# A hybrid HGRN2 / mLSTM block: where the sums and splits of the FFN operand stand, and where the HGRN stream pauses

## The chip, the cores and the metric

The kernel runs on one core of a Trainium2 chip. The core has four compute engines, each with a queue of its own that it works through in order: TensorE (PE, matrix products into PSUM banks), VectorE (DVE), ScalarE (ACT) and GpSimd (POOL). SyncE (SP) and ACT issue most DMAs. The engines wait for each other by semaphores. The metric is the time of one launch on the device in microseconds; less is better.

## The reference

One layer (DEPTH is 1) over 1024 tokens of width 1024, all in float32:

```
u = x @ w_in + b_in                       # columns split between two head groups
o_hg = rms(hgrn2(silu(hq), log_f, k, hv)) * silu(hgate)     # 4 heads, 128 x 128 state
o_ml = rms(mlstm(mq, mk, mv, ig, log_f))  * sigmoid(mo)     # 4 heads, qk 64, v 128
mix = concat(o_hg, o_ml) @ w_out
x = LN(alpha * x + mix)
ffn = (silu(x @ w_gate) * (x @ w_up)) @ w_down              # D_FF = 2816
x = LN(alpha * x + ffn)
x = x + sigmoid(x @ ple_gate + b) * (p @ ple_proj)
```

## The kernel before

**Three products for one.** A float32 product is made from two reduced halves. `split` (lines 82 to 84) rounds an operand to its high half on ACT (a cast) and takes the low half on DVE (operand minus high half). `mm3` (lines 86 to 90) then runs three matmuls, high x high (L88), high x low or low x high (L89, L90). Nearly all of PE's time lies in these three lines, and each operand costs one ACT cast and one DVE subtraction ahead of its first use.

**Stages.** `mixers` makes the projections tile by tile (`f_tile`, 2 x 24 matmuls of 512 columns into the `ft` banks) and runs the recurrences in between: generators, the "streams", hold the HGRN and the mLSTM work, and `pump` advances each stream to its next `yield` twice for every 24 matmuls. `out_proj` multiplies by w_out, normalises (`ln_rows`), transposes the result (`transposed`, PE transposes into `pt`, ACT writes `x1T`), and makes the small product p @ ple_proj (`ple_proj`: products `pp`, copied to `ppo`, sent to DRAM). `ffn_up` and `ffn_down` are the FFN.

**The HGRN stream.** `hgrn(h, b, ...)` handles head h and half b of the tokens. It makes q1 (line 527), the scores of neighbouring tokens (L533), then doubles the block length L from 2 to 64; at each length a `yield`, score products (L533 up to 16, L549 for 32 and 64), and then DVE scales q and k (L570, L571) by the decay of the block. After L = 64 come two `yield`s, the transposes of k (`pkt`, L579), the state products (`hst`, L585), the output (`po`, L599, L601), the normalisation (`rms`, which leaves `onh`), five `yield`s marked "tail", and the transposes of the output (L607). `together` runs both halves in step. `head(h)` calls `finish(head_streams[h - 1], 'tail')` after its two projections, which emits all that the former head has left up to the first "tail" at once. A head has 8 pumps between its start and that point. The score products and `po` share three PSUM banks ("hg").

**The FFN in seven products.** `ffn_up` forms the products of the 2 x 2 block matrix of x (a11, a12: the first 512 tokens, columns halves 0 and 1; a21, a22: the last 512 tokens) with sums of the weights, after Strassen and Winograd: z with A11 and A12, y with S3 and A22, x with S1 and S4, w with S2. S1 = a21 - a22, S2 = S1 - a11 (sign as in the code), S3 = a11 - a21, S4 = a12 + S2. `xs(name)` makes a sum and its split when it is first asked for; S3 is asked for ahead of the loop over the 22 weight tiles. The first four tiles' z products are made early in `out_proj` (`gate0`): z with A11, a copy to `p1` on ACT, then z goes on with A12 on the same bank, so its second half waits for that copy.

**What sets the order.** The program text is not the order of the queues: a scheduler of the tile framework places the instructions of each engine by their dependencies and by its own estimate of times. So a moved line moves its neighbours too, and the order of the built kernel is shown below where the prediction speaks of it.

Of the kernel before, what the change touches and what calls it, by code (L numbers as in the profile page):

```python
# [9 lines left out]
F32 = mybir.dt.float32  # L10
# [3 lines left out]
OP = mybir.AluOpType  # L14
# [4 lines left out]
P = 128  # L19
# [6 lines left out]
HB = 512  # L26
# [15 lines left out]
A11, A12, A22, S1, S2, S3, S4 = range(7)  # L42
# [7 lines left out]
def block_kernel(ctx, tc, a, out):  # L50
# [81 lines left out]
    with ff:  # L132
        with ExitStack() as es:
            ffn_up(g, es)
# [4 lines left out]
def mixers(g, es):  # L139
    a, act, dve, pool, pe, sp = g.a, g.act, g.dve, g.pool, g.pe, g.sp  # L140
# [30 lines left out]
    for k in range(KT):  # L171
# [7 lines left out]
        for b in range(2):  # L179
            raw = mtile("xraw")  # L180
            sp.dma_start(raw, a["xT"][:, k, b * HB:(b + 1) * HB])
            xraw.append(raw)
    for k in range(KT):
# [5 lines left out]
        for b in range(2):  # L189
            raw = xraw[2 * k + b]  # L190
# [196 lines left out]
    def rms(tag, views, scale_r):  # L387
        sq = mx.tile([P, 4, P], F32, name="sq", bufs=1)
        for sl, v in views:
            act.activation(sq[:, sl], v, AF.Square)  # L390
        ss = mx.tile([P, 4], F32, name="ss" + tag)
        dve.tensor_reduce(ss, sq, axis=AX.X, op=OP.add)
        if scale_r is not None:
            dve.tensor_mul(ss, ss, scale_r)
            dve.tensor_mul(ss, ss, scale_r)
        dve.tensor_scalar(ss, ss, 1.0 / P, RMS_EPS, op0=OP.mult, op1=OP.add)
        rs = mx.tile([P, 4], F32, name="rs" + tag)
        pool.tensor_tensor(rs, ss, g.m8[:, :4], op=OP.pow)
        if scale_r is not None:
            dve.tensor_mul(rs, rs, scale_r)  # L400
        on = mx.tile([P, 4, P], F32, name="on" + tag, bufs=1)
        for sl, v in views:
            n = len(range(4)[sl])
            dve.tensor_mul(on[:, sl], v, rs[:, sl][:, :, None].to_broadcast([P, n, P]))
        return on
# [106 lines left out]
    def hgrn(h, b, q, k, f):  # L512
        v = mx.tile([P, 4, P], F32, name="hv")
        sp.dma_start(v, g.hv_d[4 * b:4 * b + 4, :, h * P:(h + 1) * P].rearrange("c p d -> p c d"))
        k, f = (t.rearrange("p (c t) -> p c t", c=4) for t in (k, f))
# [6 lines left out]
        def odd(t):  # L522
            return t.rearrange("p c (b two) -> p c b two", two=2)[:, :, :, 1]

        A = Ab[b]
        D = mx.tile([P, 4, BK], F32, name="D")
        dve.tensor_mul(q1, odd(q), odd(f))

        def blocks(dst, rhs, n):
            for c in range(4):  # L530
                for j in range(NB):
                    s = slice(j * BK, (j + 1) * BK)
                    pe.matmul(dst[s, c], k[:, c, s], rhs[:, c, j * n:(j + 1) * n], start=True, stop=True)  # L533
# [66 lines left out]
            if prev is not None:  # L600
                pe.matmul(po[:, c], q[:, c], prev, start=False, stop=True)  # L601
        on = rms("h", [(slice(0, 4), po)], None)
        for _ in range(5):
            yield "tail"
        pt = bank("hg", [P, 4, P], "pt")
        for c in range(4):
# [33 lines left out]
def out_proj(g, es):  # L640
    a, act, dve, pool, pe, sp = g.a, g.act, g.dve, g.pool, g.pe, g.sp
    wtile, mm3, split = g.wtile, g.mm3, g.split
    lnp = es.enter_context(g.tc.tile_pool(reuse_waits="tile", name="lnp", bufs=2))
    ps = g.psC
    g.x1T = {}

    def acc_bank(name):
        return ps.tile([P, 512], F32, tag="q", bufs=8, name=name)

    mixhl = []  # L650
    for b in range(2):
        mixhl.append((g.big("mixh"), g.big("mixl")))
        for k in KORD:
            split(mixhl[b][0][:, k], mixhl[b][1][:, k], g.mix[k, b])

    g.ft = ffn_tools(g, acc_bank)
    g.early = {}

    def ple_proj(b, pw, pT):
        ph, pl = (t[:, :1024].rearrange("p (k t) -> p k t", k=2) for t in pT)  # L660
        for t in range(4):
            tt = slice(t * P, (t + 1) * P)
            for s in range(2):
                pp = acc_bank("pp")
                for k in range(2):
                    ks = slice(k * HB, (k + 1) * HB)
                    mm3(pp, (ph[:, k, tt], pl[:, k, tt]), tuple(w[:, ks] for w in pw[s]), k == 0, k == 1)
                r = g.wp.tile([P, HB], F32, name="ppo", bufs=2)
                act.copy(r, pp)
                act.dma_start(g.pp_d[4 * b + t, :, s * HB:(s + 1) * HB], r)  # L670

    def wo(b, s):
        mh, ml = mixhl[b]
        accs = [acc_bank(f"wo{t}") for t in range(4)]
        for i, k in enumerate(KORD):
            if i % 2 == 0:
                hi, lo = wtile(a["wo"][s, k // 2])
            ks = slice((k % 2) * HB, (k % 2 + 1) * HB)
            for t in range(4):
                tt = slice(t * P, (t + 1) * P)  # L680
                mm3(accs[t], (mh[:, k, tt], ml[:, k, tt]), (hi[:, ks], lo[:, ks]), i == 0, i == KT - 1)
        return accs

    def add_up(ys, s, accs):
        for t in range(4):
            hs = slice(s * HB, (s + 1) * HB)
            dve.scalar_tensor_tensor(ys[t][:, hs], ys[t][:, hs], ALPHA, accs[t], op0=OP.mult, op1=OP.add)

    def rows(b):
        ys = [lnp.tile([P, D], F32, name="y", bufs=4) for _ in range(4)]  # L690
        for t in range(4):
            act.dma_start(ys[t], a["x"][(4 * b + t) * P:(4 * b + t + 1) * P])
        return ys

    def transposed(b, ys):
        for k in range(KT):
            pt = ps.tile([P, 4, P], F32, tag="q", bufs=8, name="pt")
            for t in range(4):
                pe.transpose(pt[:, t], ys[t][:, k * P:(k + 1) * P], g.ident)
            g.x1T[k, b] = g.mtile(f"x1T{k}")  # L700
            act.activation(g.x1T[k, b], pt.rearrange("p c t -> p (c t)"), AF.Identity,
                           bias=g.ln1c[:, 1, k:k + 1], scale=g.ln1c[:, 0, k:k + 1])
        for t in range(4):
            act.dma_start(g.x1_d[4 * b + t], ys[t])

    y0 = rows(0)
    for s in range(2):
        add_up(y0, s, wo(0, s))
    for t in range(4):
        g.ln_rows(y0[t], lnp)  # L710
    accs = wo(1, 0)
    transposed(0, y0)
    y1 = rows(1)
    add_up(y1, 0, accs)
    g.X = {"A11": x_split(g, g.big("XA11"), 0, 0), "A12": x_split(g, g.big("XA12"), 4, 0)}
    accs = wo(1, 1)
    w0 = [g.ft.prep0(f) for f in range(2)]
    g.early[0] = g.ft.gate0(w0[0])
    pw = [wtile(a["wpp"][s]) for s in range(2)]
    ple_proj(0, pw, wtile(a["pT"][0]))  # L720
    w0.append(g.ft.prep0(2))
    add_up(y1, 1, accs)
    for t in range(4):
        g.ln_rows(y1[t], lnp)
    transposed(1, y1)
    pT = wtile(a["pT"][1])
    for f in range(1, 3):
        g.early[f] = g.ft.gate0(w0[f])
    ple_proj(1, pw, pT)
    g.early[3] = g.ft.gate0(g.ft.prep0(3))  # L730


def x_split(g, t, k0, b, raw=None):
    for k in range(4):
        g.split(t[:, k], t[:, 4 + k], raw[k] if raw else g.x1T[k0 + k, b])
    return t


# [45 lines left out]
def ffn_up(g, es):  # L784
    a, act, dve, sp = g.a, g.act, g.dve, g.sp
    cb = es.enter_context(g.tc.tile_pool(reuse_waits="tile", name="cb", bufs=3))
    tp = es.enter_context(g.tc.tile_pool(reuse_waits="tile", name="tp", bufs=1))
    bank = lambda name: g.psC.tile([P, HB], F32, tag="q", bufs=8, name=name)
    T, X, t = g.ft, g.X, g.x1T

    def cbt(name):
        return cb.tile([P, KT, HB], F32R, tag="cb", bufs=3, name=name)

    def row(k0, b):
        return [t[k0 + k, b] for k in range(4)]

    def comb(dst, x, y, op):
        for k in range(4):
            dve.tensor_tensor(dst[k], x[k], y[k], op=op)
        return dst  # L800

    a11, a12, a21, a22 = row(0, 0), row(4, 0), row(0, 1), row(4, 1)

    def b_s3():
        x = g.big("XS3")
        for k in range(4):
            if k % 3 == 0:
                tmp = tp.tile([P, 3, HB], F32, tag="tt", bufs=1, name="xs")
            dve.tensor_sub(tmp[:, k % 3], a11[k], a21[k])
            g.split(x[:, k], x[:, 4 + k], tmp[:, k % 3])  # L810
        return x

    def b_s1():
        return x_split(g, g.big("XS1"), 0, 1, comb(a21, a21, a22, OP.subtract))

    def b_s2():
        return x_split(g, cbt("XS2"), 0, 0, comb(a11, a21, a11, OP.subtract))

    def b_s4():
        return x_split(g, cbt("XS4"), 4, 0, comb(a12, a12, a11, OP.add))  # L820

    def b_a22():
        return x_split(g, cbt("XA22"), 4, 1)

    def xs(name):
        if name not in X:
            X[name] = {"S1": b_s1, "S2": b_s2, "S3": b_s3, "S4": b_s4, "A22": b_a22}[name]()
        return X[name]

    def wd_sums(i):  # L830
# [11 lines left out]
        act.dma_start(g.h_d[n, i], v)  # L842

    even = None
    xs("S3")
    for f in range(NF):
        gu = T.load(f)
        tt = tp.tile([P, 3, HB], F32, tag="tt", bufs=1, name="tt")
# [12 lines left out]
        y = bank("y")  # L861
# [3 lines left out]
        x = bank("x")  # L865
# [26 lines left out]
        if f % 2 == 0:  # L892
            even = h0, h1
            put(A11, i, h0)
            s3 = g.mtile("hs3")
# [259 lines left out]
```

## Time and profile before

| | us |
|---|---|
| median of the runs | 1276.87 |
| lowest run | 1275.46 |
| the profiled execution, own time | 1276.73 |
| its span (first to last instruction) | 1274.9 |
| PE idle within the span (1274.9 - 1256.3) | 18.6 |

The profile is of one execution. Its page gives busy times by engine, the chain of work that ended last and groups of instructions; other views give the waits, a timeline, or the busy time and clock in chosen stretches. A row of a timeline has the start in us, the duration in us, the engine, the line, the operation, output and inputs, shapes, a count, and in brackets the idle time before it with what ended it. A row of waits reads: engine, the waiting group, the group waited for, us in total, times, the longest. PE is the engine that is nearly always busy, so a wait of another engine costs nothing as long as it makes no wait of PE.

### The profile page before, as it was taken

How to read it: one execution, taken by the hardware profiler on the slowest of the kernel's cores; microseconds unless marked ns; L12 is line 12 of the kernel's file. 1: busy time of each engine (PE TensorE's matmuls, PEld its weight loads, DVE VectorE, ACT ScalarE, POOL GpSimd, SP SyncE). 2: the span in 40 equal slices, each digit the busy share in tenths (PEclk: the TensorE clock that was granted, in tenths of full speed). 3: DMA queues.
4: the chain of work that ended last, by engine and by line, in shares of the span. 5: the costliest groups of instructions: out<-in, count | busy, mean ns of one | idle time of the engine just before them, and what ended most of it. 6: DMA issues, size and time to landing. Idle time of an engine off the chain costs nothing.

```text
span 1274.9 us, 19256 instructions
## 1 busy us (share of the span) xinstructions
PE 1256.3 (99%) x7795; PEld 1044.1 (82%) x7795; DVE 856.9 (67%) x1444; ACT 460.4 (36%) x663; POOL 28.4 (2%) x38
## 2 busy tenths in 40 slices
PE   9999999999999999998999999999999999999998
PEld 8799888777788787877888888888888888888887
DVE  6744665566533654588978778778757875559965
ACT  4671313233322414562333333332324433434141
POOL 0000000000000000000000000000000000000000
PEclk9999999999999999999999999999999999999999
DMA  7644412111102844435554444354348876554432
GB/s 237 187 135 137 124 57 68 35 51 51 35 33 85 294 172 143 165 124 182 190 190 155 150 166 149 140 190 166 140 153 325 309 248 205 188 183 171 166 124 75
DMA packets 90025, 194.35 MB, mean 152 GB/s; under 512 B 8720, under 2 KB 29136, under 8 KB 84176
## 3 DMA queue, kind: packets, MB, share of 16 engines
q1 hardware_dynamic: 55568, 134.10, 31.3%
q10 hardware_dynamic: 34368, 59.03, 12.6%
q8 instruction: 61, 1.00, 0.3%
q14 instruction: 28, 0.23, 0.1%
HBM read 142.47 MB, written 50.63 MB: 151 GB/s over the span
## 4 chain that ended last, share of the span: by engine, by line
PE 91%; DVE 6%; issue 1%; ACT 1%; POOL 1%; DMA 0%; POOLq 0%; DVEq 0%; ACTq 0%
PE ft L88 8%; PE ft L89 7%; PE ft L90 7%; PE z L90 3%; PE z L88 3%; PE z L89 3%; PE y L90 3%; PE x L90 3%; PE y L89 3%; PE y L88 3%; PE x L89 3%; PE x L88 3%; PE dna L90 2%; PE dna L88 2%; PE pg L88 2%; PE pg L90 2%
## 5 line engine op out<-in xcount | busy, mean ns | idle before, releaser
L88 PE MATMUL ft<-xh,whl 128*128 128x512 f32 x320 | 129.2, 404 | 1.0 <-ACT k L490 1.0
L89 PE MATMUL ft<-xl,whl 128*128 128x512 f32 x320 | 127.3, 398 | 0.0
L90 PE MATMUL ft<-xh,whl 128*128 128x512 f32 x320 | 126.9, 397 | 0.0
L84 DVE TENSOR_TENSOR whl<-hw,whl 128x2048 fp32r<-128x2048 f32 (+1 forms) x42 | 88.3, 2105 | 55.4 <-ACT whl L83 55.3
L83 ACT CAST whl<-hw 128x2048 fp32r<-128x2048 f32 (+1 forms) x42 | 74.2, 1771 | 116.9 <-PE dna L90 38.5
L84 DVE TENSOR_TENSOR whl<-wraw,whl 128x1024 fp32r<-128x1024 f32 x62 | 75.2, 1218 | 51.8 <-ACT whl L83 51.8
L83 ACT CAST whl<-wraw 128x1024 fp32r<-128x1024 f32 x62 | 64.8, 1052 | 96.8 <-PE wo L90 41.8
L83 ACT CAST hl<-gu 128x1024 fp32r<-128x1024 f32 (+1 forms) x48 | 46.8, 982 | 79.3 <-PE x L90 58.9
L88 PEld LDWEIGHTS ft<-xh,whl 128*128 128x128 f32 x320 | 60.9, 190 | 15.3 <-ACT k L490 1.5
L90 PEld LDWEIGHTS ft<-xh,whl 128*128 128x128 f32 x320 | 60.1, 188 | 12.8
L89 PEld LDWEIGHTS ft<-xl,whl 128*128 128x128 f32 x320 | 60.2, 188 | 11.7
L90 PE MATMUL x<-XS,hl 128*128 128x512 f32 x176 | 69.1, 393 | 0.3 <-DVE hl L84 0.3
L89 PE MATMUL x<-XS,hl 128*128 128x512 f32 x176 | 68.9, 392 | 0.0
L88 PE MATMUL x<-XS,hl 128*128 128x512 f32 x176 | 68.9, 392 | 0.0
L90 PE MATMUL z<-XA,hl 128*128 128x512 f32 x176 | 68.6, 390 | 0.2 <-DVE hl L84 0.2
L88 PE MATMUL z<-XA,hl 128*128 128x512 f32 x176 | 68.7, 390 | 0.0
L89 PE MATMUL z<-XA,hl 128*128 128x512 f32 x176 | 68.5, 389 | 0.0
L90 PE MATMUL dna<-whl 128*128 128x512 f32 x176 | 68.5, 389 | 0.0
L88 PE MATMUL dna<-whl 128*128 128x512 f32 x176 | 68.5, 389 | 0.0
L89 PE MATMUL dna<-whl 128*128 128x512 f32 x176 | 68.5, 389 | 0.0
L83 ACT CAST hl<-tt 128x1024 fp32r<-128x1024 f32 (+1 forms) x44 | 36.8, 836 | 61.7 <-PE w L90 27.1
L84 DVE TENSOR_TENSOR hl<-gu,hl 128x1024 fp32r<-128x1024 f32 (+1 forms) x48 | 54.1, 1131 | 6.1 <-ACT hl L83 6.1
(292 smaller groups left out, 3052.6 us busy)
## 6 DMA issues: line engine op xcount, KB each, us to landing
gu<-in_wgu SPq DMA_DIRECT2D x26, 1024.0 KB, 5.1
hw<-h_d SPq DMA_DIRECT2D x35, 512.0 KB, 3.9
wdp<-in_wd SPq DMA_DIRECT2D x11, 1024.0 KB, 4.8
h_d<-hs ACTq DMA_DIRECT2D x44, 256.0 KB, 3.6
wraw<-in_wf SPq DMA_DIRECT2D x20, 512.0 KB, 3.6
hw<-w_d SPq DMA_DIRECT2D x20, 512.0 KB, 5.0
w_d<-wdp ACTq DMA_DIRECT2D x33, 256.0 KB, 2.9
wraw<-in_wo SPq DMA_DIRECT2D x16, 512.0 KB, 3.4
```

The lines of the kernel that those rows point to most:

```text
L83: g.act.copy(hi, raw)
L84: g.dve.tensor_sub(lo, raw, hi.bitcast(F32))
L88: g.pe.matmul(acc, lh, rh, start=first, stop=False, skip_group_check=more)
L89: g.pe.matmul(acc, lh, rl, start=False, stop=False, skip_group_check=more)
L90: g.pe.matmul(acc, ll, rh, start=False, stop=last, skip_group_check=more)
```

## The change

Two edits. The first: after `transposed(1, y1)` in `out_proj`, a new function `x_sums` makes S3 with its split, S1 with its split, and the sums S2 and S4 without a split. The S3 differences go through the two `ppo` buffers, which `ple_proj` also uses. In `ffn_up` only the splits of S2, S4 and A22 are left. The second: a `yield` behind q1 in `hgrn`, and four "tail" yields in place of five.

```diff
         D = mx.tile([P, 4, BK], F32, name="D")
         dve.tensor_mul(q1, odd(q), odd(f))
+        yield
...
         on = rms("h", [(slice(0, 4), po)], None)
-        for _ in range(5):
+        for _ in range(4):
             yield "tail"
...
     transposed(1, y1)
+    x_sums(g)
     pT = wtile(a["pT"][1])
...
+def x_sums(g):
+    dve, t = g.dve, g.x1T
+    row = lambda k0, b: [t[k0 + k, b] for k in range(4)]
+    a11, a12, a21, a22 = row(0, 0), row(4, 0), row(0, 1), row(4, 1)
+
+    def comb(dst, x, y, op):
+        for k in range(4):
+            dve.tensor_tensor(dst[k], x[k], y[k], op=op)
+
+    s3 = g.X["S3"] = g.big("XS3")
+    for k in range(4):
+        d = g.wp.tile([P, HB], F32, name="ppo", bufs=2)
+        dve.tensor_sub(d, a11[k], a21[k])
+        g.split(s3[:, k], s3[:, 4 + k], d)
+    comb(a21, a21, a22, OP.subtract)
+    g.X["S1"] = x_split(g, g.big("XS1"), 0, 1)
+    comb(a11, a21, a11, OP.subtract)
+    comb(a12, a12, a11, OP.add)
...
-    def b_s3():
-        x = g.big("XS3")
-        for k in range(4):
-            if k % 3 == 0:
-                tmp = tp.tile([P, 3, HB], F32, tag="tt", bufs=1, name="xs")
-            dve.tensor_sub(tmp[:, k % 3], a11[k], a21[k])
-            g.split(x[:, k], x[:, 4 + k], tmp[:, k % 3])
-        return x
-
-    def b_s1():
-        return x_split(g, g.big("XS1"), 0, 1, comb(a21, a21, a22, OP.subtract))
-
-    def b_s2():
-        return x_split(g, cbt("XS2"), 0, 0, comb(a11, a21, a11, OP.subtract))
...
     def xs(name):
         if name not in X:
-            X[name] = {"S1": b_s1, "S2": b_s2, "S3": b_s3, "S4": b_s4, "A22": b_a22}[name]()
+            X[name] = x_split(g, cbt("X" + name), *{"S2": (0, 0), "S4": (4, 0), "A22": (4, 1)}[name])
         return X[name]
...
-    xs("S3")
     for f in range(NF):
```

The order of ACT's queue behind the transposes of the second token half. Rows give line, operation, output, input and shape; `x1T7` is the last transposed tile, `wraw` to `whl` the high half of p, `z` to `p1` the copy for which the second half of z waits. Before:

```order
L701 ACTIVATE x1T7_5617<-pt_5612,c_ln1c_409 128x512
L704 DMA x1_d_69<-y_5241 128x1024
L83 CAST whl_5625<-wraw_5623 128x1024
L761 COPY p1_5641<-z_5628 128x512
L83 CAST hl2_5768<-gu_5766 128x1024
L83 CAST XS3_5808<-xs_5809 128x512
L766 ACTIVATE s0_5655<-z_5628 128x512
L761 COPY p1_5670<-z_5657 128x512
```

Now, the same place on ACT:

```order
L702 ACTIVATE x1T7_5617<-pt_5612,c_ln1c_409 128x512
L705 DMA x1_d_69<-y_5241 128x1024
L83 CAST XS3_5623<-ppo_5624 128x512
L83 CAST XS3_5623<-ppo_5628 128x512
L83 CAST XS1_5644<-x1T0_5568 128x512
L83 CAST XS1_5644<-x1T1_5575 128x512
L83 CAST whl_5663<-wraw_5661 128x1024
L83 CAST XS3_5623<-ppo_5632 128x512
L83 CAST XS3_5623<-ppo_5636 128x512
L83 CAST XS1_5644<-x1T2_5582 128x512
L83 CAST XS1_5644<-x1T3_5589 128x512
L783 COPY p1_5679<-z_5666 128x512
```

Four casts of S3 and S1 have come between the last transposed tile and the cast of p, and four more between that cast and the copy to `p1`.

The order of PE's queue at the same place, around the first `pp` products of the second half. Before:

```order
L89 MATMUL z_5657<-XA11_5250,hl2_5524 128x512
L90 MATMUL z_5657<-XA11_5250,hl2_5524 128x512
L88 MATMUL pp_5686<-whl_5429,whl_5625 128x512
L89 MATMUL pp_5686<-whl_5429,whl_5625 128x512
L88 MATMUL pp_5696<-whl_5434,whl_5625 128x512
L88 MATMUL z_5628<-XA12_5259,hl2_5395 128x512
```

Now, on PE:

```order
L89 MATMUL z_5695<-XA11_5250,hl2_5524 128x512
L90 MATMUL z_5695<-XA11_5250,hl2_5524 128x512
L88 MATMUL pp_5724<-whl_5429,whl_5663 128x512
L89 MATMUL pp_5724<-whl_5429,whl_5663 128x512
L88 MATMUL pp_5734<-whl_5434,whl_5663 128x512
L89 MATMUL pp_5734<-whl_5434,whl_5663 128x512
L88 MATMUL pp_5744<-whl_5429,whl_5663 128x512
L89 MATMUL pp_5744<-whl_5429,whl_5663 128x512
L88 MATMUL z_5666<-XA12_5259,hl2_5395 128x512
```

Six matmuls that need only the high half of p stand there instead of three, and then the second half of z as before.

The order of PE's queue where HGRN head 2 is finished (`sc` are scores, `pkt` the transposes of k, `ft` projection tiles; head 1 is alike). Before:

```order
L88 MATMUL ft_3695<-xh_91,whl_3569 128x512
L89 MATMUL ft_3695<-xl_92,whl_3569 128x512
L90 MATMUL ft_3695<-xh_91,whl_3569 128x512
L579 MATMUL pkt_3744<-c_ident_399,k_2878 128x128 x4
L579 MATMUL pkt_3751<-c_ident_399,k_2997 128x128 x4
L88 MATMUL ft_3818<-xh_89,whl_3815 128x512
```

Now, on PE:

```order
L88 MATMUL ft_3665<-xh_91,whl_3537 128x512
L89 MATMUL ft_3665<-xl_92,whl_3537 128x512
L90 MATMUL ft_3665<-xh_91,whl_3537 128x512
L550 MATMUL sc_3724<-q_3076,k_2798 64x64 x4
L550 MATMUL sc_3734<-q_3187,k_2953 64x64 x4
L580 MATMUL pkt_3744<-c_ident_399,k_2798 128x128 x4
L580 MATMUL pkt_3751<-c_ident_399,k_2953 128x128 x4
L88 MATMUL ft_3818<-xh_89,whl_3815 128x512
```

The 64-wide score products of both halves have moved from one and two groups of 12 `ft` matmuls earlier to right ahead of the transposes of k.

More of the change, by code (lines that the diff above doesn't have):

```diff
@@ L730, in out_proj, with x_split @@
     g.early[3] = g.ft.gate0(g.ft.prep0(3))
-def x_split(g, t, k0, b, raw=None):
-    for k in range(4):
-        g.split(t[:, k], t[:, 4 + k], raw[k] if raw else g.x1T[k0 + k, b])
+def x_sums(g):
[6 more added lines that the diff above has]
+    s3 = g.X["S3"] = g.big("XS3")
+    for k in range(4):
+        d = g.wp.tile([P, HB], F32, name="ppo", bufs=2)
[5 more added lines that the diff above has]
+    comb(a12, a12, a11, OP.add)
+def x_split(g, t, k0, b):
+    for k in range(4):
+        g.split(t[:, k], t[:, 4 + k], g.x1T[k0 + k, b])
     return t
@@ L788, in ffn_up @@
     bank = lambda name: g.psC.tile([P, HB], F32, tag="q", bufs=8, name=name)
-    T, X, t = g.ft, g.X, g.x1T
+    T, X = g.ft, g.X
     def cbt(name):
         return cb.tile([P, KT, HB], F32R, tag="cb", bufs=3, name=name)
-    def row(k0, b):
-        return [t[k0 + k, b] for k in range(4)]
-    def comb(dst, x, y, op):
-        for k in range(4):
-            dve.tensor_tensor(dst[k], x[k], y[k], op=op)
-        return dst
-    a11, a12, a21, a22 = row(0, 0), row(4, 0), row(0, 1), row(4, 1)
-    def b_s3():
-        x = g.big("XS3")
-        for k in range(4):
-            if k % 3 == 0:
-                tmp = tp.tile([P, 3, HB], F32, tag="tt", bufs=1, name="xs")
-            dve.tensor_sub(tmp[:, k % 3], a11[k], a21[k])
-            g.split(x[:, k], x[:, 4 + k], tmp[:, k % 3])
-        return x
-    def b_s1():
-        return x_split(g, g.big("XS1"), 0, 1, comb(a21, a21, a22, OP.subtract))
-    def b_s2():
-        return x_split(g, cbt("XS2"), 0, 0, comb(a11, a21, a11, OP.subtract))
[L819 to L823, printed above, removed]
     def xs(name):
         if name not in X:
-            X[name] = {"S1": b_s1, "S2": b_s2, "S3": b_s3, "S4": b_s4, "A22": b_a22}[name]()
+            X[name] = x_split(g, cbt("X" + name), *{"S2": (0, 0), "S4": (4, 0), "A22": (4, 1)}[name])
         return X[name]
```

## The prediction

> **What bounds the kernel now.** I read the page's busy shares first, then what TensorE (PE) waits for, then the timeline of the two places that the change touches.
>
> ```profile
> PE 1256.3 (99%) x7795; PEld 1044.1 (82%) x7795; DVE 856.9 (67%) x1444; ACT 460.4 (36%) x663; POOL 28.4 (2%) x38
> PE y L88 <- ACT hl L83: 4.4, 1, 4.4
> PE sc L549 <- DVE k L571: 1.4, 2, 0.7
> PE ft L88 <- ACT k L490: 1.0, 2, 0.5
> PE sc L533 <- DVE onh L404: 0.9, 2, 0.4
> PE sc L533 <- DVE D L557: 0.7, 1, 0.7
> PE sc L533 <- DVE k L571: 0.7, 1, 0.7
> ```
>
> PE is busy for 1256.3 of the span's 1274.9 us (from the page of before), so all its idle time is 18.6 us, or 1.5%. The change removes no matmul and adds none. It can win only a part of the waits in the lower six rows (9.1 us together) and lose what new waits it makes. The sum is therefore one of waits on PE. The first row is the start of the FFN, the other five belong to the HGRN heads.
>
> **The sums of x, first place: PE at 536 to 542 us.** The rows that price this place, from the timeline of before:
>
> ```profile
> 531.29 0.39 PE L89 MATMUL z<-XA,hl 128*128 128x512 f32 x1
> 536.28 0.39 PE L90 MATMUL z<-XA,hl 128*128 128x512 f32 x1
> 536.51 0.39 PE L88 MATMUL pp<-whl 128*128 128x512 f32 x1
> pp_d<-ppo ACTq DMA_DIRECT2D x16, 256.0 KB, 2.1
> 530.14 0.81 ACTq L670 DMA_DIRECT2D pp_d<-ppo  x2
> 531.69 3.45 ACT L701 ACTIVATE x1T<-pt,c_ln1c 128x512 f32<-128x512 f32 x5
> 535.00 1.07 ACT L83 CAST whl<-wraw 128x1024 fp32r<-128x1024 f32 x1
> 535.93 0.62 ACT L761 COPY p<-z 128x512 f32<-128x512 f32 x1
> 561.98 3.22 ACT L83 CAST XS<-x1T 128x512 fp32r<-128x512 f32 x6
> 556.02 1.89 DVE L799 TENSOR_TENSOR x1T<-x1T,x1T 128x512 f32<-128x512 f32 x3
> 536.10 1.22 DVE L84 TENSOR_TENSOR whl<-wraw,whl 128x1024 fp32r<-128x1024 f32 x1 [13.30 <-ACT whl L83]
> ```
>
> What the reader is to see: 22 steps lie between the first and second row, so a matmul follows the last every 0.227 us. The pT half `whl` is cast at 535.00 right behind the last transposed tile and is done at 536.07, so PE, which reaches `pp` at 536.51, never waits for it. An ACT cast of 512 columns follows another every (3.22 - 0.62)/5 = 0.52 us (0.62: the duration of one such cast, as in the copy row's 0.62), a DVE operation of 512 columns every 0.60 us ((1.89 - 0.68)/2, where 0.68 is one). DVE idles 13.30 us here; that is the room the change fills.
>
> In the new ACT order four casts (two of XS3, two of XS1) stand ahead of the pT cast. They run from 535.00, so that the cast starts at 535.00 + 4 x 0.52 = 537.08 and ends at 538.15. Their inputs are there: the two spill buffers `ppo` that now take the S3 differences come free 2.1 us after the issues of 530.14, at about 532.25 and 532.7, and DVE has both differences and both first sums by 534.8. PE wants `pp` at 536.5 and gets it at 538.2. **Wait one: 1.7 us.**
>
> PE then does six `pp` products (1.4 us, to 539.6) and wants the second half of z, which accumulates on the bank that ACT must first copy (`p1`). In the new ACT order that copy stands behind four more casts, the last of which needs the fourth sum of S1. That sum is DVE's 14th operation from 532.25 on (two differences, six sums, two low halves, two differences, two sums): it starts at 532.25 + 13 x 0.60 = 540.1 and ends at 540.75. One cast (0.52 to 0.6) and the copy (0.62) follow, so the copy ends at 542.0. **Wait two: 542.0 - 539.6 = 2.4 us.** Nothing covers either wait: PE runs its queue in order, and what stands behind (the `pp` low halves) waits too. The pair's lower bound is 0, if ACT reaches the two operations as early as before; the upper is 4.9, if the second buffer's write takes 2.9 instead of 2.1 us and the whole DVE chain starts that much later. I take 4.1, since each step of it is a row.
>
> **Second place: the first FFN tiles, PE at 561 to 581 us.**
>
> ```profile
> 561.50 0.59 ACT L864 COPY p<-y 128x512 f32<-128x512 f32 x1 [0.31 <-PE y L90]
> 562.63 1.90 DVE L84 TENSOR_TENSOR XS<-x1T,XS 128x512 fp32r<-128x512 f32 x3 [3.52 <-ACT XS L83]
> 574.91 0.68 DVE L851 TENSOR_TENSOR tt<-gu 128x512 f32<-128x512 f32 x1
> 575.63 1.05 ACT L83 CAST hl<-tt 128x1024 fp32r<-128x1024 f32 x1
> 576.73 0.50 PE L88 MATMUL y<-XS,hl 128*128 128x512 f32 x1 [4.39 <-ACT hl L83]
> 579.13 1.22 DVE L84 TENSOR_TENSOR hl<-tt,hl 128x1024 fp32r<-128x1024 f32 x1
> 580.53 0.51 PE L90 MATMUL y<-XS,hl 128*128 128x512 f32 x1
> ```
>
> The 4.39 us of PE come at the end of a chain on DVE. It starts when ACT gets past `p7<-y` (561.50) to the casts of S2, S4 and A22, runs without a gap from 562.63, and ends with `tt` of the second tile (574.91), whose cast lets PE go at 576.73. The S2, S4 and A22 splits aren't moved by the change: they are still made on first use. The sums which went forward had all been done before 559 us. So the chain keeps its length. It even grows: before, two of the S2 casts stood ahead of `s0<-z` on ACT and ran at 556.5; now all four stand behind `p7<-y`. From `p7<-y` to the end of `tt` there are 22 DVE operations: 0.59 + 0.55 for copy and first cast, 22 x 0.60 = 13.2 for these, 0.4 for gaps at the ends of x and y (an estimate: DVE must wait there for a product, as it did for 3.52 at 562.63 for a cast), 0.2 until ACT is free and 1.05 for the last cast: 16.0 us, where before it was 576.73 - 561.50 = 15.2. **The wait at y stays, plus 0.8.** Of that 0.4 comes back, since the low half which PE needs at 580.53 before is late by less. So this place gives +0.4, bounded by -5.0 (all of the 4.4, and 0.6 of small waits behind it, gone) and +1.5.
>
> What the clock does after a wait:
>
> ```profile
> 574.00:576.00 2.00, 0.00 (x0) 0.00 (x0) 2.00 (x4) 1.51 (x3) 0.00 (x0) 1.00 0.00 0
> 578.00:580.00 2.00, 1.66 (x4) 1.15 (x4) 2.00 (x4) 0.00 (x0) 0.00 (x0) 0.50 0.59 218
> ```
>
> After the idle 4.39 us the granted clock (third column from the right) is 0.50 for some 4 us. No idle stretch between 1.5 and 4.4 us is in the trace. For waits one and two I take full clock, the nearest idle stretches being the shorter 0.7 us of the heads, behind which the matmul rows keep their length; the other end is half clock for as long as here, about 3.4 us, which loses 1.7. The Trainium skill ("TensorE: Matmul & The Clock Gate", Part 1: The HAM clock gate) says that PE falls to half rate after an idle window of about 3.4 us, free-running, and recovers after a busy one. The 4.39 us row agrees; by the rule each of the two waits alone is too short, and only their neighbourhood could trip it.
>
> **The HGRN pause.** One pump step (12 matmuls, 2.7 us) now lies between the step that makes q1 and the first score products, one less behind the normalised output. Rows for heads 1 and 2, which are alike:
>
> ```profile
> 259.53 0.65 PE L549 MATMUL sc<-q,k 128*64 128x64 f32 x8 [0.70 <-DVE k L571]
> 268.15 0.50 PE L88 MATMUL ft<-xh,whl 128*128 128x512 f32 x1 [0.54 <-ACT k L490]
> 277.54 0.74 PE L533 MATMUL sc<-q,k 128*32 128x32 f32 x64 [0.44 <-DVE onh L404]
> 301.97 0.68 PE L549 MATMUL sc<-q,k 128*64 128x64 f32 x8
> 302.69 0.43 DVE L570 TENSOR_TENSOR q<-q,tot 128x256 f32<-128x256 f32 x1 [1.51 <-PE sc L549]
> 303.03 0.42 DVE L571 TENSOR_TENSOR k<-k,tot 128x256 f32<-128x256 f32 x1
> 305.47 1.03 PE L579 MATMUL pkt<-c_ident,k 128*128 128x128 f32 x8
> ```
>
> Gains, each twice: the 0.70 between 32- and 64-wide scores (12 matmuls now stand there), the 0.44 for the bank that `onh` frees (17 matmuls now stand ahead of the scores instead of 5), and half of the 0.54 at ft, since what I add next runs ahead of it. Together 2 x (0.70 + 0.44 + 0.27) = 2.8. Loss, twice: the k transposes now stand right behind both 64-wide products. k is ready 303.45 - 301.97 = 1.5 us after the first product starts, and the two products take 1.2: wait 0.3. The second block's k comes 0.9 later, the first transposes cover 0.5: wait 0.4. Together 1.4. Head 0 loses its two waits of 0.7 in part, since its first scores get 24 short matmuls more room: I take 0.2 of 1.4, with both ends from 1.4 gained to 0.7 lost. The sum is -2.8 + 1.4 - 0.2 = **-1.6**, between -4.7 (all five rows of HGRN waits in the first fence gone and none new) and +1.5 (the loss without a gain). The queues of SP and POOL keep their order of work; nothing there is put ahead of a load that PE waits for.
>
> **The sum.** 4.1 + 0.4 - 1.6 = +2.9 us on the profiled execution's own 1276.73 us (span 1274.9 and 1.8 around it), 0.14 under the median of the runs shown. That gives 1279.6.
>
> **Rivals.**
> - *Faster*: the sums leave DVE so free that the chain behind `p7<-y` no longer decides, and the first two waits are hidden. Then 4.9 of the second place and 1.6 of the heads go: 1276.73 - 6.5 = 1270.2. For it: DVE idles 13.30 us at 536 us. Against it: the chain has 22 DVE operations between two events that are 10.9 us of PE work (48 matmuls) apart; it decides as long as it is longer than 10.9 us, and it is 16. Chance 0.08.
> - *The early waits are hidden, the late one stays*: if the ACT casts come to the pT cast before 536.5. Then 1276.73 + 0.4 - 1.6 = 1275.5. For it: before, ACT had 0.4 us to spare there. Against it: four casts are 2.1 us. Chance 0.13.
> - *Half clock*: waits one and two lie 1.4 us apart, so that 1.4 of 5.5 us are busy. If that slows the clock: 1279.6 + 1.7 = 1281.3. Chance 0.10.
> - *The pause costs*: the transposes wait as worked out and the gains don't come, since the released DVE work only waits elsewhere: +1.5 instead of -1.6, 1282.7. Chance 0.09.
>
> **How the numbers follow.** My forecast has 0.60; its own range is 1277 to 1282. The range of 8 in 10 leaves out the faster rival (0.08) and about 0.1 of tails: 1274 to 1284. A measurement of this kernel can tell about 2% (25 us) from no change. All cases lie within 7 us, so faster by over 2% has 0.01, slower by over 2% has 0.02 (a second chain of waits that I have not seen), and within 2% has 0.97.
>
> **What would show it.** Right: the waits of PE list `pp` behind ACT `whl` with 1.5 to 2 us and `z` behind ACT `p` with 2 to 3, the y row behind ACT `hl` still at 3 to 5, `sc` behind `onh` and behind k gone, and `pkt` behind DVE k with about 0.3 to 0.4 four times. Wrong: a y wait under 1 us, or a PE wait list of HGRN that is longer than before; or PE idle below 16 us in all.

## The result

The changed kernel takes 1286.84 us in the median of 4 runs (1285.92 to 1287.71), beside 1276.78 us for the kernel before on the same chip: a ratio of 1.008, with a 95% interval of 1.0068 to 1.0092. That is slower by 10 us, beyond the predicted range. One of the four executions of the kernel before was disturbed (1780.70 us), as was the profiled one of `h_only` below (2527.29 us); the ratios leave such executions out. The profiled execution took 1285.92 us (span 1284.1, before 1274.9).

The busy shares and the waits of PE in the kernel after, the same two views as before. In the second list the columns are the time waited in all, how often, and the longest.

```profile
PE 1259.6 (98%) x7795; PEld 1044.8 (81%) x7795; DVE 858.6 (67%) x1444; ACT 460.2 (36%) x663; POOL 27.8 (2%) x38
PE z L88 <- ACT p L783: 5.0, 2, 3.9
PE y L88 <- ACT hl L83: 3.7, 1, 3.7
PE pkt L580 <- DVE k L572: 1.8, 4, 0.5
PE ft L88 <- DVE q L504: 1.8, 2, 0.9
PE pp L88 <- ACT whl L83: 1.6, 1, 1.6
PE sc L534 <- DVE k L572: 1.0, 2, 0.8
```

Every engine does as many instructions as before. The list has the rows that the prediction named, and two that it did not: `ft` behind `q`, and a second wait of `z` behind `p` (two times, 5.0 us together). `sc` behind k, which was to go, is left with 1.0 us, 0.8 of it in head 0.

Where the 9.2 us of span came in can be read from the starts of the same event in both traces. The first pair of transposed tiles reaches ACT at 527.11 instead of 528.19 (1.1 us earlier; at the first product of the output projection, right behind the HGRN heads, it is 0.8, at 417.46 instead of 418.26). The first `pp` product starts at 537.15 instead of 536.51 (0.6 later), the y product of the second FFN tile at 585.41 instead of 576.73 (8.7 later), and the lag at 629 us is 9.1; from there on it stays. So the whole loss lies in less than 100 us around the start of the FFN.

The timeline of the kernel after at the first place, ACT, DVE and PE in order of time (start, duration, engine, line, what; in brackets how long the engine stood idle and who released it):

```profile
527.11 1.45 ACT L702 ACTIVATE x1T<-pt,c_ln1c 128x512 f32<-128x512 f32 x2 [2.42 <-PE pt L700]
529.07 0.81 ACTq L671 DMA_DIRECT2D pp_d<-ppo  x2
532.97 1.32 DVE L747 TENSOR_TENSOR ppo<-x1T,x1T 128x512 f32<-128x512 f32 x2 [11.31 <-DMA pp_d<-ppo]
536.05 1.04 ACT L83 CAST whl<-wraw 128x1024 fp32r<-128x1024 f32 x1
537.15 0.50 PE L88 MATMUL pp<-whl 128*128 128x512 f32 x1 [1.56 <-ACT whl L83]
539.74 1.22 ACT L83 CAST XS<-ppo 128x512 fp32r<-128x512 f32 x2 [2.65 <-DVE ppo L747]
542.07 0.58 ACT L783 COPY p<-z 128x512 f32<-128x512 f32 x1
542.71 0.80 PE L88 MATMUL z<-XA,hl 128*128 128x512 f32 x1 [3.91 <-ACT p L783]
```

The reader is to see the chain: two spill stores are issued at 529.07, and DVE can write the S3 differences into their buffers only at 532.97, 3.9 us later. ACT, which has to cast those differences in its order, idles 2.65 us for them, and behind these casts stands the copy to `p1` for which PE waits 3.91 us.

The clock after that wait, in windows of 2 us (columns: length, PE busy and instructions, granted clock, DMA share, GB/s):

```profile
542.00:544.00 2.00, 1.29 (x3) 0.64 0.00 0
544.00:546.00 2.00, 2.00 (x6) 0.50 0.00 0
546.00:548.00 2.00, 2.00 (x11) 1.00 0.00 0
```

Eight matmuls run at half speed there: from 542.71 to 546.15 they take 3.4 us instead of 1.8.

The third place, which the prediction had not seen, some 20 us later:

```profile
549.84 6.36 SPq L767 DMA_DIRECT2D gu<-in_wgu  x2
557.20 0.33 ACTq L671 DMA_DIRECT2D pp_d<-ppo  x1
562.26 0.59 ACT L670 COPY ppo<-pp 128x512 f32<-128x512 f32 x1 [5.08 <-DMA pp_d<-ppo]
564.28 0.59 ACT L783 COPY p<-z 128x512 f32<-128x512 f32 x1 [0.40 <-ACT ppo L670]
564.92 0.50 PE L88 MATMUL z<-XA,hl 128*128 128x512 f32 x1 [1.12 <-ACT p L783]
```

The second weight load of 1 MB (the second of the two issues in the first row, about 556 us) now runs while the spill stores of the PLE projection are still being written. ACT stands still for 5.08 us on a spill buffer, and the next `p1` copy stands behind it. Before, the last of these stores was issued at 556.06 us.

### The profile page after: what moved, and what is told of

It reads as the page before. It is cut to its first block, busy times and chain, and to the rows that moved or that the text cites. A ratio compares the mean times of both kernels' runs of the same rounds, so it can differ in the third digit from the quotient of the medians.

```text
span 1284.1 us, 19261 instructions
## 1 busy us (share of the span) xinstructions
PE 1259.6 (98%) x7795; PEld 1044.8 (81%) x7795; DVE 858.6 (67%) x1444; ACT 460.2 (36%) x663; POOL 27.8 (2%) x38
## 4 chain that ended last, share of the span: by engine, by line
PE 90%; DVE 6%; ACT 2%; issue 1%; DMA 1%; POOL 0%; ACTq 0%; DVEq 0%; POOLq 0%
PE ft L88 7%; PE ft L89 7%; PE ft L90 7%; PE z L88 3%; PE y L90 3%; PE y L88 3%; PE z L90 3%; PE y L89 3%; PE z L89 3%; PE x L88 3%; PE x L89 3%; PE x L90 3%; PE pg L88 2%; PE dna L90 2%; PE dna L88 2%; PE dna L89 2%
```

## The experiments

**One part alone.** Two kernels take the two parts of the change apart. The first has the HGRN edits and nothing of x:

```
         dve.tensor_mul(q1, odd(q), odd(f))
+        yield
...
-        for _ in range(5):
+        for _ in range(4):
             yield "tail"
```

> Theory A (the HGRN pause gains a little: the trace of the change reaches the transposes of x 1.1 us earlier than before): 1275.7 us, 1.1 under the kernel before; PE waits for k at pkt 1.8 and for q at ft 1.8 in total, none at onh; the y wait at the FFN start 4.4 as before and no wait at pp. Rival B (the pause costs, and part of the 10 us is its doing): 1279 or more, with other waits in the heads.

Measured: 1276.08 us against 1276.71, ratio 0.9991 [0.9981, 1.0]. (No rows of it are shown.) The second is the change without these two edits:

> Theory A (all of the loss is the sums of x): 1287.5 us, that is the change without the HGRN gain of 1.1; PE waits pp 1.6, z about 4 with half clock behind it, a second z wait of about 1, y 3.7. Rival B (the pause has part of the loss): 1283 or less.

Measured: 1286.41 us, ratio 1.0071 [1.0055, 1.0088]. The sums of x are the loss. The pause alone measures about 1 us (0.0009 x 1276), with an interval that just reaches nothing, and inside the change it does not show: the change without it stands at 1.0071, with it at 1.008.

**The order on ACT.** In `z_first` the pT half and the gate products of tiles 1 and 2 are asked for ahead of the sums:

```
+    pT = wtile(a["pT"][1])
+    for f in range(1, 3):
+        g.early[f] = g.ft.gate0(w0[f])
     x_sums(g)
-    pT = wtile(a["pT"][1])
-    for f in range(1, 3):
-        g.early[f] = g.ft.gate0(w0[f])
     ple_proj(1, pw, pT)
```

> The change, but with the load and split of p and the two early z products written ahead of the sums; the S3 differences stay in the ppo buffers. Theory A (the loss comes from casts and copies that stand behind the sums on ACT, and the differences wait for the ppo writes): no wait at pp, none at the first z copy, 1.8 us at the second z copy, which still stands behind a cast that needs a ppo buffer; y 3 to 4; 1278. Rival C (the loss is DVE's load by the sums, wherever they stand): still 1284 or more.

Measured: 1277.25 us, ratio 1.0004 [0.9995, 1.0013]. The same sums and splits, as early on DVE, cost nothing once ACT makes the cast and the copies that PE wants first. The wait at `pp` is gone, and the two waits of `z` are 1.3 us each, where none and 1.8 had been expected. Its waits from 520 to 640 us:

```profile
PE y L88 <- ACT hl L83: 3.0, 1, 3.0
PE z L88 <- ACT p L783: 2.6, 2, 1.3
```

In `pt_first` only the pT line is moved ahead of the sums:

> The change, with the pT half asked for ahead of the sums of x, and nothing else. On ACT the cast of pT then stands ahead of all casts of XS3 and XS1, and the p1 copy behind four of them instead of eight. Theory A (each wait comes from the ACT order, and each casts' place counts): no wait at pp, z waits 0.5 to 1.5 us, no half clock: 1279 to 1281. Theory B (the two waits trade, since the DVE chain sets the end of both): no wait at pp, z waits 5 to 5.5, half clock as before: 1286 to 1287.

Measured: 1281.12 us (1277.21 to 1283.64, 10 runs), ratio 1.0034 [1.0022, 1.0046], just above the range of theory A. The waits did not trade: its profile, of an execution of 1277.83 us, has 2.4 us at the low half of `pp` (a wait that I had not expected, behind DVE) and 0.9 at `z`. The spread of 6 us is wide. The runs above 1282 us show a mean granted clock of 0.995 to 0.996, those below 1278 us 0.998. A stretch of 3.4 us at 0.50 takes 0.0013 off this mean (an estimate, 1.7 / 1276), so the longer runs may have had one or two such stretches more; no trace of one was kept.

**A buffer of its own for the differences.** Since DVE waits for the spill buffers, `z_own` is `z_first` with the S3 differences in a weight buffer that is free at that time:

```
+    xd = g.fw.tile([P, 4, HB], F32, tag="gu", bufs=3, name="xd")
     for k in range(4):
-        d = g.wp.tile([P, HB], F32, name="ppo", bufs=2)
+        d = xd[:, k]
```

> As z_first, and the four S3 differences go to a buffer of their own (one of the weight buffers) instead of the two ppo buffers. Theory A: DVE starts with the differences at about 528 instead of 533, no wait at pp or z; y 3 to 4; 1275.5. Rival C (DVE's load): 1284 or more. Rival D (the ppo buffers don't matter, only the order): the same as z_first within 0.5 us.

Measured: 1283.64 us, ratio 1.0052 [1.0037, 1.0067]: a miss of theory A, and near the number of rival C, but for another reason than DVE's load. Taking one of the three weight buffers moved two 1 MB weight loads to 520 and 527 us, on top of the spill stores of the first half. Rows of `z_own` from 520 us on:

```profile
520.33 7.52 SPq L768 DMA_DIRECT2D gu<-in_wgu  x2
527.58 1.22 ACT L670 COPY ppo<-pp 128x512 f32<-128x512 f32 x2 [5.93 <-DMA pp_d<-ppo]
534.01 1.22 ACT L670 COPY ppo<-pp 128x512 f32<-128x512 f32 x2 [3.35 <-DMA pp_d<-ppo]
534.65 0.50 PE L88 MATMUL z<-XA,hl 128*128 128x512 f32 x1 [3.28 <-ACT ppo L670]
```

ACT waited 5.93 and 3.35 us for these stores, and PE for ACT. It is the same collision as at the third place of the change. What a spill store takes is thus no constant: 2.1 us in the median of the kernel before, 5.6 to 6.5 us under a weight load here and at the third place.

**Why the two stores land late.** At 529 us no weight load is under way, and yet the two stores took 3.7 and 3.9 us. The trace of before has the same pair at 530.14, and read at that place it says 4.4 us too, not the median of 2.1. The DMA views of before (issues from 530 to 531 us, then from 524 to 527 us: how many, KB each, median us to landing) and of after (528 to 534 us, queues and issues):

```profile
pp_d<-ppo ACTq DMA_DIRECT2D x2, 256.0 KB, 4.4
...
pp_d<-ppo ACTq DMA_DIRECT2D x2, 256.0 KB, 2.1
```

```profile
q10 hardware_dynamic: 430, 1.04, 45.3%
q8 instruction: 1, 0.02, 1.4%
issues: line engine op xcount, KB each, median us to landing
pp_d<-ppo ACTq DMA_DIRECT2D x2, 256.0 KB, 3.8
x_d<-y ACTq DMA_DIRECT2D x1, 512.0 KB, 4.4
```

Two things share the time with the pair: a 512 KB store of y behind it, and one load of instructions on queue q8. `x_late` moves the store of y behind the first gate products:

```
-        for t in range(4):
-            act.dma_start(g.x1_d[4 * b + t], ys[t])
+        if b == 0:
+            stored(0, ys)
...
+    stored(1, y1)
     ple_proj(1, pw, pT)
```

> The change, with the stores of the second half's rows y to x1_d asked for behind the first gate products instead of right behind the transposes (one 512 KB store moves from 530 to about 540 us; one XS1 cast also slips behind the p1 copy). In the changed kernel the two spill buffers that take the S3 differences come free 3.7 and 3.9 us after their stores are issued, where most such stores take 2.1. Theory A (the 512 KB store behind them takes their share of the DMA engines): they land after 2.1, DVE starts at issue + 2.1 to 2.5, the wait of z behind the p1 copy falls from 3.9 to 1.6 to 2.2, the half clock behind it goes: 1282 to 1283.5 us. Theory B (that store has nothing to do with it): landing stays at 3.7 to 4.4, the wait of z falls only by the one cast, to 3.3, and the time is 1286 to 1287.

Measured: 1285.92 us, ratio 1.0069 [1.0053, 1.0086]. The pair, alone now, landed after 4.5 us: theory A falls. (The z wait was 1.95 us, shorter than theory B said, but `pp` waited 2.2 before it, and the clock fell between the two.) The view of 528 to 534 us of `x_late` shows how the two stores end; the first row is the rate in 40 slices of 0.15 us:

```profile
GB/s 0 0 0 0 0 68 287 355 382 396 342 314 396 492 328 28 0 0 0 14 0 14 14 14 27 14 27 27 27 27 14 0 0 0 0 0 0 0 0 0
DMA packets 289, 0.54 MB, mean 90 GB/s; under 512 B 32, under 2 KB 32, under 8 KB 288
...
q8 instruction: 1, 0.02, 1.0%
```

Nearly all bytes are through after 1.5 us at some 400 GB/s. The rest trickles at 14 to 27 GB/s for another 2 us. 400 / 16 is 25, so this looks like one DMA engine of 16 that is late with its share.

That leaves the load of instructions. The page of after has 61 loads on q8, 1.00 MB, and PE has 7795 matmuls and as many weight loads: 15590 / 61 = 256 instructions a load. So q8 most likely brings PE's instructions, and the loads should shift with a few more PE instructions at the start, as they then did. `i_shift` and `i_shift2` do that, for the rest they are the change. `i_shift` has 24 fp32 products of 8 columns instead of one of the two warming products; the edit of `i_shift2`:

```
-    for _ in range(2):
-        pe.matmul(wb, warm[:, :P], warm, start=True, stop=True)
+    wh = warm.bitcast(mybir.dt.bfloat16)
+    for _ in range(48):
+        pe.matmul(wb[:, :64], wh[:, :P], wh[:, :64], start=True, stop=True)
```

> The change, with 24 more tiny fp32 matmuls (8 columns) in place of one of the two warming ones at the start, which shifts every later block of PE instructions. In all traces so far one 16 KB instruction load lies in the same microsecond as the two late spill stores at 530 us. Theory B1 (the instruction load holds the stores back): the load moves away by some 10 us, the two stores land after 2.1 to 2.5, the wait of z is 1.6 to 2.4 and the half clock behind it is gone: 1283 to 1285 us, the start costing 0 to 2 us. Theory B2 (the load is harmless): landing stays 3.7 to 4.4, the z wait 3.5 to 3.9, time 1286 to 1289.

Measured: 1293.61 us, ratio 1.0137 [1.0122, 1.0152], outside of both theories, since the tiny fp32 products put off the first real product from 4.77 to 13.45 us. From the first `pp` product (9.2 us later than in the change) to the end (6.8 later) it gained 2.4 us. The pair landed in time, DVE starting 2.3 us after the issue; the z wait was 2.33 us with a full clock behind it. Without the price at the start:

> The shift of the PE instruction blocks again, without its price at the start: the change with 48 tiny bfloat16 matmuls (64 columns) in place of the two warming fp32 ones, which ends before the first operands are there. The blocks lie 44 matmul and weight-load pairs earlier, about as in the first shift (46). Theory B1 (the instruction load holds back the spill stores that share its time): the pair of stores behind the S3 differences lands after 2.0 to 2.5 us, another pair is late instead, the z wait is 2.0 to 2.5, no half clock behind it: 1283 to 1285 us (the first shift got 2.4 back from the pp row to the end). Theory B2 (the first shift was luck): landing 3.6 to 4.5, z wait 3.5 to 3.9, 1286 to 1288.

Measured: 1283.13 us, ratio 1.005 [1.0035, 1.0065]. Rows of `i_shift2`: the pair behind the S3 differences, the z wait, the clock behind it (columns as above), then the DMA view of 521 to 525 us.

```profile
528.77 0.82 ACTq L672 DMA_DIRECT2D pp_d<-ppo  x2
531.07 1.33 DVE L748 TENSOR_TENSOR ppo<-x1T,x1T 128x512 f32<-128x512 f32 x2 [9.71 <-DMA pp_d<-ppo]
540.81 0.50 PE L88 MATMUL z<-XA,hl 128*128 128x512 f32 x1 [2.33 <-ACT p L784]
542.00:543.00 1.00, 1.00 (x4) 0.50 0.00 0
```

```profile
q8 instruction: 1, 0.02, 1.8%
issues: line engine op xcount, KB each, median us to landing
pp_d<-ppo ACTq DMA_DIRECT2D x2, 256.0 KB, 3.7
x_d<-y ACTq DMA_DIRECT2D x1, 512.0 KB, 4.6
```

The load of instructions now meets an earlier pair, and that pair is the one that takes 3.7 us; the pair behind S3 lands in 2.3. Shifted twice, by 46 and by 44 pairs, the load met this earlier pair both times (3.6 and 3.7 us in `i_shift`), and the delay went with it. One thing came out otherwise than expected: the clock still fell to 0.50 a microsecond after the z wait of 2.33 us, so the gain at this place lies in the wait (3.91 to 2.33; at the third place, 1.12 to 0.60) and not in the clock. Behind y the clock was back after 3.4 us at 0.50, instead of 6.8.

**The late chain.** The change left the splits of S2, S4 and A22 where they were. Two kernels ask for them ahead of the FFN loop; `h_eager` is the kernel before with the HGRN pause moved, `eager_only` has nothing else:

```
-    xs("S3")
+    for n in ("S3", "S1", "S2", "S4", "A22"):
+        xs(n)
     for f in range(NF):
```

> The kernel before with the HGRN pause moved, and the splits of S1, S2, S4 and A22 asked for ahead of the loop over the FFN tiles, so that on ACT all their casts stand ahead of the copy p7 of the first tile. It is the part that the change left out: theory A (the 4.4 us at y of the second tile are the length of a DVE chain that starts when ACT gets past p7): the y wait falls under 1.5 us with its half clock: 1270 to 1272.5 us. Theory B (the splits wait for memory that the output projection frees, so that they start no earlier): the y wait stays at 3.5 to 4.5, 1276 to 1277.5.

Measured: 1272.35 us (1272.14 to 1272.53), ratio 0.9969 [0.9957, 0.9981]. The waits of PE from 520 to 640 us in `h_eager`, which makes its FFN products in another order too:

```profile
PE x L88 <- DVE p L869: 1.3, 2, 0.7
PE z L88 <- ACT p L762: 0.7, 1, 0.7
PE y L88 <- ACT hl L83: 0.2, 1, 0.2
```

The 4.4 us at y are 0.2, and in every window of 2 us from 536 to 596 us the clock is 1.00.

> The kernel before with the splits of S1, S2, S4 and A22 asked for ahead of the loop, and nothing else; the HGRN pause is where it was. If the pause is worth what it measured alone (0.9991, about 1 us) and the two parts add, 1272.8 to 1274 us; if the pause was worth nothing, 1272.2 to 1272.6, the same as with both.

Measured: 1273.31 us, ratio 0.997 [0.9957, 0.9982]: that is in the range that speaks for a pause worth 1 us, but the intervals of the two ratios overlap, so the pause stays undecided at this size.

> The whole change with the two things put right that the runs so far point to: the pT half and the gate products of tiles 1 and 2 asked for ahead of the sums of x, and the splits of S2, S4 and A22 asked for ahead of the FFN loop. Theory A (the early waits come from the ACT order, the late one from the casts behind p7, and the two cures add): y wait under 1.5 us, no half clock there, 1271 to 1273.5 us. Theory B (with the sums early, the late chain is bound by memory that the output projection frees): y wait 2.5 to 3.5 and 1276 to 1277.5.

Measured: 1275.95 us, ratio 0.9994 [0.9984, 1.0003]: half a miss. The y wait went as theory A has it (0.4 us), yet the time is that of theory B. What remains are waits that `h_eager` has less of, 2.7 us at `z` (0.7 there) and 1.7 at `x` (1.3):

```profile
PE z L88 <- ACT p L783: 2.7, 2, 1.4
PE x L88 <- DVE p L859: 1.7, 3, 0.7
```

The two kernels differ in where S3, S1 and the sums are made. Early, they keep ACT and DVE busy while PE wants its `p1` copies, even when the first of these stand ahead of them; by the two ratios that costs about 0.0025 x 1276 = 3.2 us.

## Why the prediction failed

The direction was right, and so was the mechanism of the first two waits; the size was not: +2.9 us forecast, +9.2 in the profiled span. Step by step:

| step | predicted us | measured us |
|---|---|---|
| HGRN pause | -1.6 | -1.1 |
| wait one, `pp` behind the pT cast | 1.7 | 1.6 |
| wait two, `z` behind the `p1` copy | 2.4 | 3.9 |
| half clock behind it | 0 (a rival: 1.7) | 1.6 |
| third place, `z` behind a spill buffer | not seen | 1.1 |
| the first FFN tiles | 0.4 | 1.3 |
| not in these rows | | 0.8 |

Of the 0.8, some 0.5 is a matter of counting. Products start every 0.227 us and each lasts 0.39, so each of the three waits puts the next start off by 0.16 or 0.17 us more than the idle time listed.

- **The term that failed first is wait two.** "The two spill buffers `ppo` that now take the S3 differences come free 2.1 us after the issues of 530.14": 2.1 is the median over 16 stores, and the pair at 530.14 itself took 4.4 us in the trace of before. The prediction quoted that very issue and priced it by the median of its group. With 3.9 us to landing, the DVE chain starts 1.8 us later and the wait is 3.9 instead of 2.4. Waits one and two came to 5.5 us together, above the upper bound of 4.9, since that allowed 2.9 us for a landing. `i_shift2`, where DVE starts 2.3 us after the issue, has 2.33 us, which is the predicted 2.4. Yet this term alone does not mend the forecast: the span of `i_shift2` is still 6.1 us longer than before (1281.0). The rest lies in the steps that follow.
- **The half clock was a rival at 0.10 and came true.** The Trainium skill ("TensorE: Matmul & The Clock Gate", Part 1: The HAM clock gate) gives an idle window of about 3.4 us, free-running, behind which PE is at half rate. The runs agree in part: at these places each stretch at 0.50 lasted 3.41 us or two or three times that, and no wait of 3.5 us and more went without one. But shorter waits cost the clock too. Those of 1.1 to 1.6 us kept 1.00, and those between went either way: 3.28 us in `z_own` and 3.01 in `z_first` lost it, 2.90 in `z_own` did not, and 2.33 us kept full clock in `i_shift` and lost it in `i_shift2`. So "each of the two waits alone is too short" does not hold here for waits of 2.3 us and more. The prediction also asked the rule only about the wait it had computed; at the named bound of 4.9 us for the pair, 3.2 for wait two alone, the rival would have had a much larger chance.
- **The third place was missed**, because the prediction followed ACT's new order only up to the second `p1` copy. Once PE is 6 us late, the PLE projection's stores slip under the weight load. (Before, only the last store did, and no product waited for it.)
- **The first FFN tiles** were right in the chain: from `p7` to the y product it took 16.1 us, forecast 16.0, before 15.2.

```profile
569.33 0.59 ACT L854 COPY p<-y 128x512 f32<-128x512 f32 x1 [0.76 <-PE y L90]
585.41 0.80 PE L88 MATMUL y<-XS,hl 128*128 128x512 f32 x1 [3.75 <-ACT hl L83]
```

The y wait itself is shorter than before (3.75 us, before 4.39), since the twelve products on A22 just ahead of it take 4.0 us instead of 2.5: the low halves of the split come late. What failed is the 0.4 that was to come back behind y. The clock stays at 0.50 until 5.0 us after the y product started, before until 4.0, and from that product to the first `w` product of the tile 8.0 us pass instead of 7.6. That the chain behind `p7` sets this place, `h_eager` shows.

- **HGRN** came near its number, but in part by luck. The waits of heads 1 and 2 that were to go are gone, and `pkt` waits 0.44 to 0.48 us four times (0.3 to 0.4 predicted). The step missed a new wait, `ft` behind `q`, 0.93 and 0.88 us where 0.54 and 0.48 had been, and of that 0.27 was to go each time. The waits listed for the heads are thus 4.6 us together, before 4.7, and do not make a gain of 1.1. Of the 0.8 us at the first product of the output projection, PE's idle time gives 0.3 (7.8 us up to there, before 8.1) and its busy time 0.5; the other 0.3 came within the output projection, which the pause does not touch. No run shows why.

The rival "early waits hidden" failed on the order of ACT that the prediction had read; `z_first`, which alters that order, comes near its time. The rival "faster" failed as argued: the chain behind `p7` still decided, in `z_first` too, with 3.0 us at y. The rival "the pause costs" is not borne out: `h_only` is not slower than the kernel before (0.9991, at most 1.0).

## What to carry to other kernels

Price a DMA that a new wait hangs on by its own row at its own place, not by the median of its group: one store of 256 KB took 2.1, 4.4 or 6.1 us, depending on what else was moving. When work is brought forward on an engine that runs its queue in order, look for what then stands behind it and what stands behind that, until the lateness is gone; a wait of 2 to 3 us can cost its clock as well (here every wait of 3.0 us or more met a half clock). And move what the chain of waits ends on: here the splits behind `p7`, not the sums that had long been done.

## What the runs showed of the hardware

A 16 KB load of instructions, one for every 256 of PE's, held back the pair of 256 KB stores that it met. In twelve traces (all but that of `h_only`) one such load falls on a pair of spill stores between 520 and 535 us, and that pair took 3.6 to 4.5 us (but for one single store of `z_first`, 2.5), where its neighbours took 2.0 to 2.6 unless a weight load ran; when the load was shifted, another pair was the late one. Every spill store in these traces that took more than 2.7 us met such a load or a weight load. Single spill stores further on that met such a load, and no weight load, took 2.1 to 3.2 us, so the delay is not the same everywhere. Nearly all of the bytes of the pair in `x_late` were through after 1.5 us, and what remained came at the rate of one DMA engine in 16; which one, and why it loses 2 us over 16 KB, no run here shows. The Trainium skill ("Runtime: NRT & Kernel Launch", Instruction fetch mechanics) has blocks of 16 KiB or 256 instructions, which the counts here agree with, and calls the cost of crossing one mostly hidden. For PE that holds, since all its idle time in the kernel before is 18.6 us, with 61 loads; for a store on whose buffer another engine waits it does not.
